# A two-layer hybrid decoder trunk: where the modulation's dots and the softmax sums stand in the order of work

## The chip, the cores and the metric

The kernel runs on one core of a Trainium2 chip. The metric is the device time of one execution in microseconds; the median over several runs counts. Three runs of the kernel before gave 1451.97, 1452.05 and 1452.85 us.

TensorE (PE) multiplies, and transposes by multiplying with the identity. VectorE (DVE) and ScalarE (ACT) do everything between the products. SyncE (SP) issues most of the transfers, GpSimd (POOL) those that add weights in flight. Each engine works off its own queue in order and waits for the others by semaphores.

## The reference

Two layers, 512 positions, width 1024, all in f32. A vector `c` modulates every layer with six vectors of width 1024 (shift, scale and gain, for the mixers and for the feed-forward).

```python
mod = silu(c) @ w_ada + b_ada
sh1, sc1, g1, sh2, sc2, g2 = jnp.split(mod, 6, axis=-1)
h = rmsnorm(x, norm1_w) * (1 + sc1) + sh1
u = h @ w_in                       # pool, conv (u, b, c), q, k, v, three gates
...
o = moba_attention(q, k, v)        # 8 heads of 64, blocks of 256, causal
merged = (gates[:, :, 0] * (y_pool @ p_pool) + gates[:, :, 1] * (y_conv @ p_conv)
          + gates[:, :, 2] * (y_attn @ p_attn))
x = x + g1 * (merged @ w_out)
h2 = rmsnorm(x, norm2_w) * (1 + sc2) + sh2
x = x + g2 * ((silu(h2 @ w_gate) * (h2 @ w_up)) @ w_down)
```

`w_ada` is 1024 by 6144 in each layer. The feed-forward is 2816 wide.

## The kernel before

**Tiling.** Activations lie with features on the 128 partitions and the 512 positions along the free dimension, so a vector of width 1024 is eight tiles. Every f32 product is three matmuls (`mm3`, L159) of a high and a low part: weights arrive by DMA in a raw tile of eight 128 x 128 blocks, ACT rounds them to the high part (`whi`, L327), VectorE subtracts to get the low part (`wlo`, L330). `next_w` (L351) keeps three or four such weight tiles ahead of the one in use. There are three raw buffers, five each of `whi` and `wlo`, and six of a general 4 KB kind, `w4`.

**Stages of a layer.** Input projection; pooling and convolution; K and V; then the attention, which runs in between the products of the first two gates; the third gate and the merging (`GATE2`, with steps "gate j" and "attn j"); the output projection (`tail`, L981); the feed-forward in four parts (`PARTS`), each gate and up products, some of them in pairs (`glu_pair`, L1077) whose weights are sums made by POOL's accumulating transfers into `w4` tiles (`Sums`, L240), and then the down projection, column by column, each ending in a `residual` (L977), `x += product * gain`.

**Dots.** The modulation is not a matmul. For each of the six vectors and each of its eight columns, SP fetches a 128 x 1024 tile of `w_ada` (512 KB) and VectorE multiplies it with silu(c) and sums along the row (`ada_step`, L398, the instruction at L376). `ada_end` (L405) adds the bias to a whole vector. The dots of shift 1 and scale 1 of layer 0 run at the start; the others are tasks with a cost of 1.2 each (0.2 for an `ada_end`) in a queue, `bulk`.

**Order.** Nothing is scheduled at run time: the order of the program is written by three helpers. `mm3` counts columns, and after each 2048 of them (four products of 512 columns) it calls `tick` (L135). A tick steps every fiber that is due and then gives `bulk` a credit of `bulk_rate`; credit is capped at 4.0, and while it is not negative, tasks are taken and charged. `flush_bulk` takes what is left at once. Instructions under `pin` (or `keep_in_program_order`) keep their order; the rest may be moved by the compiler where data and buffers allow. All matmuls, dots and weight splits are pinned.

**Attention.** A fiber, `attention` (L681), goes through four pairs of heads. For each it transposes Q and K (`to_features`) and starts four units, one for each block of 128 queries, `GAP` ticks apart. A `unit` (L582) computes scores, mask, maxima and exponentials, for blocks 2 and 3 separately for keys before and in their own block of 256 (L619 to L639), adds the two sums (L640), takes the reciprocal (L641) and scales the exponentials (L643). After `WAIT` ticks it transposes them and splits the transposes (L654, L655), two ticks later it multiplies with V, and reads the product out (L669 to L674). `tick` steps the attention fiber ahead of the units, as it is first in the list.

**Where the dots stand before.** In layer 0: shift 2 and scale 2 amid the attention, at a rate of 0.27 and in raw buffers (`early=True`); gain 2 in the output projection, at 0.9; then `DOTS = (8, 8, 2, 0)` tasks of layer 1's 36 (scale 1, shift 1, scale 2, shift 2) in the down projections of parts 0 to 3, five more in the last one's tail, and 13 in layer 1's input projection. In layer 1: gain 2 in the output projection. `dots_after` keeps a dot behind the last split of the pair before it.

Of the kernel before, what the change touches and what calls it, by code (L numbers as in the profile page):

```python
# [25 lines left out]
KT = D // P  # L26
# [9 lines left out]
BLOCK = 256  # L36
# [11 lines left out]

SUMS_AHEAD = 4

DOTS = (8, 8, 2, 0)

RAW, BIG = 3, 46

# [25 lines left out]
def hybrid_trunk(ctx, tc, xT, ws, ada, cols, pool_w, qk_w, crow, pos, con, out):  # L80
# [52 lines left out]
            bulk.popleft()[1]()  # L133

    def tick():  # L135
        for f in list(fibers):
            f[0] -= 1
            if f[0] <= 0:
                n = next(f[1], None)
                if n is None:  # L140
                    fibers.remove(f)
                else:
                    f[0] = n
        run_bulk(bulk_rate[0])

    def drain():
        while fibers:
            tick()
# [256 lines left out]
    def ada_end(l, part):  # L405
# [4 lines left out]
        if part == G1:  # L410
            V.tensor_scalar(m, m, 0.5, None, op0=ALU.mult)

    def ada_tasks(l, parts, early=False):
        out = []
        for part in parts:
            for j in range(KT):
                out.append((1.2, lambda part=part, j=j: ada_step(l, part, j, early)))
            out.append((0.2, lambda part=part: ada_end(l, part)))
        return out
# [162 lines left out]
    def unit(hp, i, q, k, v, y, nrq, prq):  # L582

        w = P * (i + 1)

        def scores(o, i, n):
            for z, (qa, ka) in enumerate(((0, 0), (0, 1), (1, 0))):
                for a in range(2):
                    r = slice(a * HD, (a + 1) * HD)
                    matmul(o[:, a], q[qa][r, i * P:(i + 1) * P], k[ka][r, :n], start=(z == 0), stop=(z == 2))  # L590


        if i == 0:
            s = first_two[hp] = ps_pair()
            for u in range(2):
                scores(s[:, :, u * BLOCK:(u + 1) * BLOCK], u, BLOCK)
            diag = s.rearrange("p a (g c) -> p a g c", c=P)[:, :, 0:TT:TT - 1]
            V.tensor_add(diag, diag, mask.unsqueeze(1).unsqueeze(1).to_broadcast([P, 2, 2, P]))
        elif i == 1:
            s = first_two.pop(hp)[:, :, BLOCK:]  # L600
        elif i == 2:

            s, last_one[hp] = ps_pair(), ps_pair()
            for u, o in ((2, s), (3, last_one[hp])):
                scores(o[:, :, :(u + 1) * P], u, (u + 1) * P)
        else:
            s = last_one.pop(hp)
        cell = lambda: sm([P, 2], tag="asm", bufs=16)
        nsc, sc = nrq[:, i, 2 * hp:2 * hp + 2], prq[:, i, 2 * hp:2 * hp + 2]
        m, nb, den = cell(), cell(), cell()  # L610
        pr = [tmp() for _ in range(2)]
        if w <= BLOCK:
            V.tensor_reduce(m, s[:, :, :w], axis=AX.X, op=ALU.max)
            V.tensor_mul(nb, m, nsc)
            for a in range(2):
                A.activation(pr[a][:, :w], s[:, a, :w], AF.Exp, bias=nb[:, a:a + 1],
                             scale=sc[:, a:a + 1], accum_out=den[:, a:a + 1])
        else:

            past, own, diag = s[:, :, :BLOCK], s[:, :, BLOCK:w], s[:, :, i * P:w]  # L620
            gs, under, mp, nbp, d2 = cell(), cell(), cell(), cell(), cell()
            V.tensor_reduce(gs, past, axis=AX.X, op=ALU.add)  # L622
            V.tensor_reduce(mp, past, axis=AX.X, op=ALU.max)  # L623
            for a in range(2):
                V.scalar_tensor_tensor(under[:, a:a + 1], gs[:, a:a + 1], sc[:, a:a + 1], fill,
                                       op0=ALU.mult, op1=ALU.is_lt)
            V.tensor_add(diag, diag, mask.unsqueeze(1).to_broadcast([P, 2, P]))
            V.scalar_tensor_tensor(mp, under, NEG, mp, op0=ALU.mult, op1=ALU.add)
            V.tensor_reduce(m, own, axis=AX.X, op=ALU.max)  # L629
            for a in range(2):  # L630
                V.scalar_tensor_tensor(nb[:, a:a + 1], m[:, a:a + 1], mp[:, a:a + 1], nsc[:, a:a + 1],
                                       op0=ALU.max, op1=ALU.mult)
            V.scalar_tensor_tensor(nbp, under, NEG, nb, op0=ALU.mult, op1=ALU.add)
            for a in range(2):
                A.activation(pr[a][:, BLOCK:w], own[:, a], AF.Exp, bias=nb[:, a:a + 1],  # L635
                             scale=sc[:, a:a + 1], accum_out=den[:, a:a + 1])
            for a in range(2):
                A.activation(pr[a][:, :BLOCK], past[:, a], AF.Exp, bias=nbp[:, a:a + 1],  # L638
                             scale=sc[:, a:a + 1], accum_out=d2[:, a:a + 1])  # L639
            V.tensor_add(den, den, d2)  # L640
        V.reciprocal(den, den)  # L641
        for a in range(2):
            V.tensor_scalar(pr[a][:, :w], pr[a][:, :w], den[:, a:a + 1], None, op0=ALU.mult)  # L643
        yield WAIT[i]

        pt = [None] * 2
        for aa in ([0, 1],) if i < 2 else ([0], [1]):
            n = len(aa)
            tp = ps_mm().rearrange("p (j a q) -> p j a q", a=n, q=P)[:, :i + 1]
            for a in aa:  # L650
                for j in range(i + 1):
                    transpose(tp[:, j, a - aa[0], :], pr[a][:, j * P:(j + 1) * P], ident)
            both = w4([P, i + 1, n, 2, P], F32R)
            A.activation(both[:, :, :, 0], tp, AF.Copy)  # L654
            V.tensor_sub(both[:, :, :, 1], tp, f32(both)[:, :, :, 0])  # L655
            for a in aa:
                pt[a] = both[:, :, a - aa[0]]
        yield 2


        po = (s[:, 0] if i >= 2 else ps_mm()).rearrange("p (a h q) -> p a h q", a=2, h=2)
        for a in range(2):
            for j in range(i + 1):
                matmul(po[:, a].rearrange("p h q -> p (h q)"), v[hp // 2][j][:, hp % 2 * 2 + a].rearrange("p h d -> p (h d)"),
                       pt[a][:, j].rearrange("p h q -> p (h q)"), start=(j == 0), stop=(j == i))
        c = slice(i * P, (i + 1) * P)
        t = tmp()
        part, total = t[:HD, :2 * P].rearrange("p (a q) -> p a q", a=2), t[:, 2 * P:3 * P]
        A.activation(part, po[HD:, :, 0], AF.Copy)  # L669
        V.tensor_add(part, part, po[:HD, :, 1])  # L670
        for a in range(2):
            V.tensor_add(total[a * HD:(a + 1) * HD], part[:, a], po[:HD, a, 0])
        A.activation(y[0][:, c], total, AF.Copy)
        V.tensor_sub(y[1][:, c], total, f32(y[0])[:, c])  # L674
# [65 lines left out]
    for l in range(L):  # L740
# [7 lines left out]
        for n, (k, lo, hi) in enumerate([(k, 0, S) for k in range(KT)] if l == 0 else HALVES + REST):  # L748
# [12 lines left out]
                held[k] = next_w(0 if l == 0 else None)  # L761
            if l > 0 and n == 1:
                second(norm, l, 0, bank)
                bulk.extend(later)
                bulk_rate[0] = 0.75
            w = held[k]
            h = norm.k(k)
            for t in range(lo // P, hi // P):
# [152 lines left out]
            mm3(pp, (pw["h"][:, j, :], pw["l"][:, j, :]), pooled[j], True, True)  # L921
            y_pool.append(split_from(pp, scale=col(C_PS + j)))

        if l == 0:
            bulk.extend(ada_tasks(l, (SC2, SH2), True))
        bulk_rate[0] = 0.27
        ahead_now[0] = 3

        def gate():
# [29 lines left out]
        for step, j in GATE2:  # L959
            if step == "gate":  # L960
                sg2[j] = gate()
                continue
            if j == 0:
                drain()
            if j % 2 == 0:
                aw_ = next_w()
            p1 = ps_mm()
            for z in range(PAIRS):
                mm3(p1, wblk(aw_, 4 * (j % 2) + z), y_attn[z], z == 0, z == PAIRS - 1)
            t = sg2.pop(j)  # L970
            gated(t, p1)
            V.tensor_add(t, t, m01[j])
            merged.append(split_from(t))
        flush_bulk()


        def residual(k, src, lo, hi, part):  # L977
# [50 lines left out]
            return go  # L1028

        ahead_now[0] = 4  # L1030
        bulk.extend(ada_tasks(l, (G2,)))
        bulk_rate[0] = 0.9
        n2 = Norm()
        n2.h = [bigt(F32) for _ in range(KT)]
        table(AF.Abs_reciprocal_sqrt, t[:, 0:1])
# [91 lines left out]
        for part, (along, single, pairs) in enumerate(PARTS):  # L1127
# [25 lines left out]
            bulk_rate[0] = 0.0  # L1153
            for p in range(pairs):
                glu_pair(p == pairs - 1)
            if l + 1 < L:
                if part == 0:
                    later = ada_tasks(l + 1, (SC1, SH1, SC2, SH2))
                n = DOTS[part]
                bulk.extend(later[:n])  # L1160
                del later[:n]
            bulk_rate[0] = 1.5
            blk = Blocks(nk, 4)
            if part + 1 < len(PARTS):
                for n in range(KT):
                    if n == KT // 2:
                        bulk_rate[0] = 0.0
                    o = ps_mm()
                    for k in range(nk):
                        mm3(o, blk(n, k), act[k], k == 0, k == nk - 1)  # L1170
                    residual(n, o, 0, S, G2)
            elif l + 1 == L:
                tail(lambda k: act[k], blk, G2, nk, None, True)
            else:
                flush_bulk()
                drain()
                bulk.extend(later[:5])
                del later[:5]
                bulk_rate[0], credit[0] = 0.8, 0.0
                n1 = Norm()  # L1180
                table(AF.Abs_reciprocal_sqrt, f32(act[-1][1])[:, 0:1])
# [104 lines left out]
```

## Time and profile before

| | us |
|---|---|
| median of three runs | 1452.05 |
| the profiled execution | 1453.0 |
| its span, first to last instruction | 1451.2 |
| PE, matmuls busy | 1442.0 |
| PE, weight loads busy | 1264.8 |
| DVE busy | 1063.1 |
| ACT busy | 663.5 |
| POOL busy | 105.2 |

The stages, by the times from the span's start: input projection of layer 0 from 24, attention and gates 126 to 303, merging 303 to 339, output projection to 388, feed-forward to 726; layer 1's input projection to 799, its attention 838 to 1018, its output projection from 1055, its feed-forward from 1104 to the end.

In the rows of the timeline the columns are: start, busy time, engine, line, operation, output and inputs, shapes, how many instructions were merged, and in brackets the idle time of the engine before it with what ended it. Matmuls overlap, so the distance from one start to the next is their pace, not their busy time. In the rows of the chain the columns are start, length and what it was.

### The profile page before, as it was taken

To read this page: it belongs to the slowest core of one execution; us is meant where nothing else is said; L and a number is where in the kernel's file an instruction comes from. 1 tells how busy PE (TensorE), PEld (TensorE's weight loads), DVE (VectorE), ACT (ScalarE), POOL (GpSimd) and SP (SyncE) were. 2 spreads that over 40 slices of the span, in tenths; PEclk is the share of its full clock that TensorE was granted. 3 is DMA by queue.
4 is the path that set the end of the run, shared out by engine and by line. 5 is a ranking of instruction groups with operands and counts; after the bars stand their busy time and mean duration, and the time that the engine had idled before them with its cause. 6 is when DMAs were issued, how large, how long until landed. Compare 5 with 4: busy or idle time off the path is not lost.

```text
span 1451.2 us, 21838 instructions
## 1 busy us (share of the span) xinstructions
PE 1442.0 (99%) x8379; PEld 1264.8 (87%) x8379; DVE 1063.1 (73%) x1879; ACT 663.5 (46%) x1138; POOL 105.2 (7%) x157
## 2 busy tenths in 40 slices
PE   9999999999999999999999999999999999999998
PEld 7888788888988998989988877888889989989997
DVE  7987888858686767677797776776577757657663
ACT  4634555533553452535444355555335525534450
POOL 0000000001100311210000000000020102111200
PEclk9999999999999999999999999999999999999999
DMA  9644333364436767756545422223473436636432
GB/s 352 223 141 167 124 115 104 117 217 152 100 132 213 196 174 205 187 153 195 190 147 178 151 87 73 73 73 109 153 200 90 135 113 175 174 106 185 131 92 83
DMA packets 84409, 217.18 MB, mean 150 GB/s; under 512 B 10832, under 2 KB 23760, under 8 KB 84304
## 3 DMA queue, kind: packets, MB, share of 16 engines
q1 hardware_dynamic: 67456, 177.37, 35.9%
q0 software_dynamic: 16128, 37.76, 11.8%
q8 instruction: 65, 1.06, 0.3%
q10 hardware_dynamic: 720, 0.66, 0.1%
q14 instruction: 40, 0.33, 0.1%
HBM read 213.65 MB, written 2.10 MB: 149 GB/s over the span
## 4 chain that ended last, share of the span: by engine, by line
PE 92%; DVE 5%; DMA 1%; ACT 1%; issue 1%; SPq 0%; ACTq 0%; DVEq 0%
PE mm L151 78%; PE pair L151 12%; PE mm L157 1%; DVE wlo L330 1%; DMA w<-in_ada 1%; DVE w L376 0%; DVE raw L376 0%; DMA x<-in_xT 0%; DMA raw<-in_ws 0%; DVE tmp L643 0%; DVE asm L622 0%; ACT tmp L638 0%; DVE asm L629 0%; DVE asm L623 0%; ACT tmp L635 0%
## 5 line engine op out<-in xcount | busy, mean ns | idle before, releaser
L151 PE MATMUL mm<-big,whi 128*128 128x512 f32 (+1 forms) x4362 | 1080.2, 339 | 1.7 <-DVE big L938 0.9
L151 PEld LDWEIGHTS mm<-big,whi 128*128 128x128 f32 x4362 | 745.2, 190 | 87.2 <-DVE big L938 1.5
L151 PE MATMUL mm<-big,wlo 128*128 128x512 f32 (+1 forms) x2181 | 736.1, 338 | 0.0
L151 PEld LDWEIGHTS mm<-big,wlo 128*128 128x128 f32 x2181 | 413.8, 190 | 44.5
L327 ACT ACTIVATE whi<-raw 128x1024 fp32r<-128x1024 f32 (+2 forms) x240 | 248.9, 1040 | 265.7 <-PE mm L151 190.2
L330 DVE TENSOR_TENSOR wlo<-raw,whi 128x1024 fp32r<-128x1024 f32 (+2 forms) x240 | 283.9, 1192 | 50.5 <-ACT whi L327 47.7
L327 ACT ACTIVATE whi<-w 128x1024 fp32r<-128x1024 f32 x72 | 76.2, 1058 | 148.1 <-PE mm L151 85.3
L978 DVE SCALAR_TENSOR_TENSOR x<-mm,mod,x 128x512 f32<-128x512 f32 (+1 forms) x90 | 61.7, 689 | 78.1 <-PE mm L151 77.9
L256 POOL DMA_DIRECT2D w<-in_ws x72 | 46.3, 656 | 951.6 <-issue 294.1
L330 DVE TENSOR_TENSOR wlo<-w,whi 128x1024 fp32r<-128x1024 f32 x72 | 86.7, 1221 | 31.6 <-ACT whi L327 30.9
L376 DVE SCALAR_TENSOR_TENSOR w<-w,csil 128x1024 f32<-128x1024 f32 x80 | 95.9, 1220 | 16.9 <-DMA w<-in_ada 16.8
L151 PE MATMUL pair<-whi,big 128*128 128x512 f32 x224 | 76.8, 390 | 0.0
L258 POOL DMA_DIRECT2D w<-in_ws x72 | 64.0, 897 | 157.8 <-DMA w<-in_ws 142.6
L151 PE MATMUL pair<-big,whi 128*128 128x256 f32 (+1 forms) x376 | 74.0, 294 | 0.0
L151 PEld LDWEIGHTS pair<-big,whi 128*128 128x128 f32 x376 | 60.4, 191 | 2.2
L151 PE MATMUL mm<-whi,big 128*128 128x512 f32 x160 | 57.2, 394 | 1.4 <-ACT big L501 1.1
L151 PE MATMUL pair<-big,wlo 128*128 128x256 f32 (+1 forms) x188 | 55.3, 294 | 0.0
L938 DVE SCALAR_TENSOR_TENSOR big<-big,mm 128x512 f32<-128x512 f32 x48 | 32.5, 683 | 28.6 <-PE mm L151 28.5
L151 PEld LDWEIGHTS pair<-whi,big 128*128 128x128 f32 x224 | 42.1, 188 | 8.8
L515 DVE TENSOR_TENSOR big<-tmp,big 128x512 fp32r<-128x512 f32 x48 | 33.1, 691 | 21.4 <-ACT big L514 20.4
L514 ACT ACTIVATE big<-tmp 128x512 fp32r<-128x512 f32 x48 | 29.9, 622 | 36.2 <-DVE tmp L1120 12.8
L151 PE MATMUL pair<-wlo,big 128*128 128x512 f32 x112 | 43.6, 390 | 0.0
(190 smaller groups left out, 1238.5 us busy)
## 6 DMA issues: line engine op xcount, KB each, us to landing
raw<-in_ws SPq DMA_DIRECT2D x146, 512.0 KB, 3.3
w<-in_ada SPq DMA_DIRECT2D x80, 512.0 KB, 4.9
w<-in_ws POOLq DMA_DIRECT2D x144, 256.0 KB, 4.7
raw<-in_ws SPq DMA_DIRECT2D x64, 256.0 KB, 3.8
raw<-in_ws SPq DMA_DIRECT2D x24, 384.0 KB, 3.5
raw<-in_ada SPq DMA_DIRECT2D x16, 512.0 KB, 3.3
raw<-in_ws SPq DMA_DIRECT2D x16, 448.0 KB, 5.1
raw<-in_ws SPq DMA_DIRECT2D x36, 128.0 KB, 2.8
```

Source lines behind the costliest of these rows:

```text
L151: tc.keep_in_program_order(T.matmul(*a, **k))
L157: tc.keep_in_program_order(T.transpose(*a))
L256: nc.gpsimd.dma_start(dst, self.source(0, 1))
L258: nc.gpsimd.dma_start(dst, self.source(*other), accum_op=ALU.add)
L327: A.activation(hi[:, :n], raw[:, :n], AF.Copy)
L330: ins = V.tensor_sub(lo[:, :n], raw[:, :n], f32(hi)[:, :n])
L376: return V.scalar_tensor_tensor(aw, aw, 1.0, csil, op0=ALU.mult, op1=ALU.mult, accum_out=mod[l][:, part, j:j + 1])
L514: A.activation(hi, src, AF.Copy)
L515: last_split[0] = V.tensor_sub(lo, src, f32(hi))
L938: V.scalar_tensor_tensor(sg, sg, 1.0, branch, op0=ALU.add, op1=ALU.mult)
L978: V.scalar_tensor_tensor(x[k][:, lo:hi], src, mod[l][:, part, k:k + 1], x[k][:, lo:hi], op0=ALU.mult, op1=ALU.add)
```

## The change

Four things. The dots of shift 2 and scale 2 leave layer 0's attention and layer 1's input projection; in both layers they start with the step "attn 0" of the merging, behind `drain`, at a rate of 0.85 and in `w4` buffers, and run on into the output projection. The dots of gain 2 leave the output projection; in both layers they become single columns, `g2_column`, each with its own bias add on ACT: three behind the pair of feed-forward part 0 and one ahead of each of the next five columns of its down projection. With 18 tasks of layer 1 instead of 36, `DOTS` becomes (0, 9, 4, 0), and the last five go into the last tail. In a unit for query blocks 2 and 3, two ticks pass between the exponentials and L640 (now pinned), and one instead of three between the scaling and the transposes. `tick` serves the first fiber, the attention, last.

```diff
-DOTS = (8, 8, 2, 0)
+DOTS = (0, 9, 4, 0)
...
     def tick():
-        for f in list(fibers):
+
+        for f in fibers[1:] + fibers[:1]:
             f[0] -= 1
...
+    def g2_column(l, j):
+
+        ada_step(l, G2, j, False)
+        m = mod[l][:, G2, j:j + 1]
+        A.activation(m, m, AF.Identity, bias=colt[:, l, C_ADA + G2 * KT + j:C_ADA + G2 * KT + j + 1])
...
                 A.activation(pr[a][:, :BLOCK], past[:, a], AF.Exp, bias=nbp[:, a:a + 1],
                              scale=sc[:, a:a + 1], accum_out=d2[:, a:a + 1])
-            V.tensor_add(den, den, d2)
+
+            yield 2
+            pin(V.tensor_add(den, den, d2))
         V.reciprocal(den, den)
         for a in range(2):
             V.tensor_scalar(pr[a][:, :w], pr[a][:, :w], den[:, a:a + 1], None, op0=ALU.mult)
-        yield WAIT[i]
+        yield WAIT[i] - (2 if w > BLOCK else 0)
...
                 second(norm, l, 0, bank)
-                bulk.extend(later)
-                bulk_rate[0] = 0.75
...
-        if l == 0:
-            bulk.extend(ada_tasks(l, (SC2, SH2), True))
-        bulk_rate[0] = 0.27
+        bulk_rate[0] = 0.0
         ahead_now[0] = 3
...
             if j == 0:
                 drain()
+                bulk.extend(ada_tasks(l, (SC2, SH2)))
+                bulk_rate[0] = 0.85
...
             merged.append(split_from(t))
-        flush_bulk()
...
         ahead_now[0] = 4
-        bulk.extend(ada_tasks(l, (G2,)))
-        bulk_rate[0] = 0.9
...
                 glu_pair(p == pairs - 1)
+            if part == 0:
+                for j in range(3):
+                    g2_column(l, j)
             if l + 1 < L:
                 if part == 0:
-                    later = ada_tasks(l + 1, (SC1, SH1, SC2, SH2))
+                    later = ada_tasks(l + 1, (SC1, SH1))
...
                         bulk_rate[0] = 0.0
+                    if part == 0 and n + 3 < KT:
+                        g2_column(l, n + 3)
                     o = ps_mm()
...
                 flush_bulk()
                 drain()
-                bulk.extend(later[:5])
-                del later[:5]
+                bulk.extend(later)
```

## The prediction

> **What bounds the kernel now.** I read the page first, its busy shares, costliest groups and DMA issues, then the windows by stage, then the timeline at each place where TensorE shows a pause.
>
> ```profile
> span 1451.2 us, 21838 instructions
> PE 1442.0 (99%) x8379; PEld 1264.8 (87%) x8379; DVE 1063.1 (73%) x1879; ACT 663.5 (46%) x1138; POOL 105.2 (7%) x157
> ...
> L376 DVE SCALAR_TENSOR_TENSOR w<-w,csil 128x1024 f32<-128x1024 f32 x80 | 95.9, 1220 | 16.9 <-DMA w<-in_ada 16.8
> w<-in_ada SPq DMA_DIRECT2D x80, 512.0 KB, 4.9
> ```
>
> TensorE is the bound, and its matmuls are untouched by the change. So VectorE work is worth nothing by itself; only those places count where TensorE stands still for it. A dot (L376) costs 1.22 us of VectorE and a transfer of 512 KB, 4.9 us from issue to landing. The windows by stage (columns: length, then busy time of PE, PEld, DVE, ACT, POOL, then clock, DMA share, GB/s) say where such places can be:
>
> ```profile
> 126.00:303.00 177.00, 176.06 (x913) 144.30 (x912) 144.10 (x336) 92.72 (x211) 0.00 (x0) 1.00 0.38 127
> 303.00:339.00 36.00, 36.00 (x161) 29.79 (x160) 22.56 (x33) 11.96 (x17) 0.00 (x0) 1.00 0.47 168
> 339.00:388.00 49.00, 49.00 (x273) 42.96 (x272) 35.92 (x59) 18.81 (x29) 8.75 (x12) 1.00 0.56 158
> 749.00:795.00 46.00, 46.00 (x205) 38.08 (x204) 36.86 (x59) 18.43 (x27) 0.31 (x1) 1.00 0.56 196
> 838.00:1018.00 180.00, 178.39 (x922) 145.58 (x921) 128.51 (x308) 95.47 (x215) 0.00 (x0) 1.00 0.25 86
> ```
>
> In the two attention stages (126 to 303 and 838 to 1018) TensorE loses 0.94 and 1.61 us by this count; in the merging (303 to 339), the output projection behind it, and the input projection of layer 1 (749 to 795) it loses nothing. The change can gain in the attention alone, a few microseconds at most. Everywhere else it can only lose.
>
> **What it removes.** Layer 0's wait, seen in the timeline:
>
> ```profile
> 145.44 1.22 DVE L376 SCALAR_TENSOR_TENSOR raw<-raw,csil 128x1024 f32<-128x1024 f32 x1
> ...
> 159.03 0.75 DVE L643 TENSOR_SCALAR tmp<-tmp,asm 128x384 f32<-128x384 f32 x2
> ...
> 160.86 0.49 PE L157 MATMUL mm<-ident,tmp 128*128 128x128 f32 x3
> ...
> 161.22 0.57 DVE L672 TENSOR_TENSOR tmp<-tmp,mm 64x128 f32<-64x128 f32 x2
> ...
> 161.94 0.52 PE L157 MATMUL mm<-ident,tmp 128*128 128x128 f32 x3 [0.58 <-DVE tmp L672]
> ...
> 162.81 0.74 PE L151 MATMUL mm<-big,whi 128*128 128x512 f32 x2 [0.35 <-ACT big L933]
> ```
>
> Six transposes take from 160.86 to 162.81, 1.95 us. Their second half needs a PSUM buffer that L672 has to read out first, and the next matmul one that ACT's L933 frees, itself queued behind what follows L672. VectorE is late because it is hardly idle from the dot at 145.44 on. Layer 1, without dots, runs the same piece in 875.47 - 874.90 = 0.57 us (next fence). So the first term is 1.95 - 0.57 = 1.38 us. The second half is late by 161.94 - 160.86 - 0.57 / 2 = 0.8 us. The dot taken out (1.22) is more than that alone, and L643 (0.75) moves too, so I take the whole of it.
>
> Layer 1's waits:
>
> ```profile
> 874.90 0.81 PE L157 MATMUL mm<-ident,tmp 128*128 128x128 f32 x6
> ...
> 875.47 0.70 PE L151 MATMUL mm<-big,whi 128*128 128x512 f32 x2
> ...
> 876.24 0.62 PE L151 MATMUL mm<-big,whi 128*128 128x512 f32 x2
> ...
> 876.71 0.40 PE L151 MATMUL mm<-big,wlo 128*128 128x512 f32 x1
> ...
> 877.17 0.16 DVE L640 TENSOR_TENSOR asm<-asm,asm 128x2 f32<-128x2 f32 x1 [1.91 <-ACT tmp L638]
> 877.25 0.68 DVE L938 SCALAR_TENSOR_TENSOR big<-big,mm 128x512 f32<-128x512 f32 x1
> ...
> 877.98 0.73 PE L151 MATMUL mm<-big,whi 128*128 128x512 f32 x2 [0.88 <-DVE big L938]
> 878.55 0.40 PE L151 MATMUL mm<-big,wlo 128*128 128x512 f32 x1
> ...
> 960.99 0.16 DVE L640 TENSOR_TENSOR asm<-asm,asm 128x2 f32<-128x2 f32 x1 [0.70 <-ACT tmp L638]
> ...
> 961.95 0.60 PE L157 MATMUL mm<-ident,w 128*128 128x128 f32 x4
> 962.18 1.02 DVE L655 TENSOR_TENSOR w<-mm,w 128x384 fp32r<-128x384 f32 x2
> ...
> 962.79 0.72 PE L151 MATMUL mm<-big,whi 128*128 128x512 f32 x2 [0.24 <-DVE w L655]
> ```
>
> This is the wait that the delayed sum is made for. L640 stands at the head of VectorE's queue for 1.91 us, until ACT's exponentials (L638) are done; L938 stands behind it, and a matmul needs the buffer that L938 frees. The pace without a wait is (876.71 - 876.24) / 2 = 0.235 us a matmul, here it is 877.98 - 876.71 = 1.27: a loss of 1.03. The pair behind the wait is slow too: 878.55 - 877.98 = 0.57 against 0.47, another 0.10. At 962 it is the same pattern: L640 waits 0.70, L641 and L643 run behind it, and L655, which frees the transposes' buffer, comes late. Four transposes take 0.84 (961.95 to 962.79); undisturbed they take 0.38:
>
> ```profile
> 839.83 0.63 PE L157 MATMUL mm<-ident,w 128*128 128x128 f32 x4 [0.27 <-DVE big L909]
> ...
> 840.21 0.70 PE L151 MATMUL mm<-big,whi 128*128 128x512 f32 x2
> ```
>
> a loss of 0.46. Sum removed: 1.38 + 1.03 + 0.10 + 0.46 = 2.97 us. The wait for L909 in this last fence belongs to the evacuation of V and is not touched.
>
> **What it adds and moves.** (a) *Sums two steps later.* No instruction is added. A step is four mm3 calls, 12 x 0.235 = 2.8 us of TensorE; the sums keep one step ahead of the transposes that need them, and last 962.18 - 960.99 = 1.2 us, from L640 to what follows L643. The pinned L640 then waits for exponentials issued two steps ago, so it is ready, and the weight splits behind it do not wait. Cost 0 if VectorE is less than 2.8 - 1.2 = 1.6 us behind its program at that step; if it is further behind, rival 1. Serving old units first moves their transposes ahead of new scores inside one step: nothing by itself, the condition is the same.
>
> (b) *16 dots into the merging, both layers.* VectorE has room early and none late there:
>
> ```profile
> 316.05 3.72 DVE L330 TENSOR_TENSOR wlo<-raw,whi 128x1024 fp32r<-128x1024 f32 x3
> 325.79 0.69 DVE L938 SCALAR_TENSOR_TENSOR big<-big,mm 128x512 f32<-128x512 f32 x1 [6.02 <-PE mm L151]
> ...
> 331.23 1.22 DVE L330 TENSOR_TENSOR wlo<-raw,whi 128x1024 fp32r<-128x1024 f32 x1
> ...
> 339.38 0.69 DVE L938 SCALAR_TENSOR_TENSOR big<-big,mm 128x512 f32<-128x512 f32 x1 [0.17 <-PE mm L151]
> ...
> 340.82 1.37 DVE L515 TENSOR_TENSOR big<-big,big 128x512 fp32r<-128x512 f32 x2
> ```
>
> The credit of the bulk queue is at its cap of 4.0 when the dots enter (rate 1.4 with an empty queue before), so with a cost of 1.2 a dot and a rate of 0.85 a step four dots fall into the first step, one each into steps 2, 4 and 5, and with attn 2 to 7 (steps 7 to 12) come steps 7, 8, 10 and 11, four more; the last five fall into the first columns of the output projection, where the eight G2 dots that stood there are gone. The dots of steps 1 to 8 can run in the idle time before 325.79 (6.02 us). The two of steps 10 and 11 follow the split at 331.23, where VectorE is full: 2 x 1.22 = 2.44 us. Behind them stands L515 of column 7, which ends at 340.82 + 1.37 = 342.2. TensorE ends attn 7 at 339.4, and reads that tile's low half after seven products of three matmuls and one matmul more, 22 x 0.227, at 344.4 (the pace is from the chain's rows in (c)). The slack is 2.2, so 0.24 us is lost. Lower bound 0 (dots run earlier), upper bound all four in the full stretch: 4.9 - 2.2 = 2.7. I take 0.3 a layer, 0.6 in all, because the tick arithmetic is fixed by the code.
>
> (c) *G2 dots as single columns in feed-forward part 0.* Four are pinned ahead of the splits of the third to fifth weight tile:
>
> ```profile
> 451.09 0.69 DVE L515 TENSOR_TENSOR big<-tmp,big 128x512 fp32r<-128x512 f32 x1 [0.70 <-ACT big L514]
> 451.70 3.48 DVE L330 TENSOR_TENSOR wlo<-raw,whi 128x1024 fp32r<-128x1024 f32 x3
> 455.11 1.22 DVE L376 SCALAR_TENSOR_TENSOR w<-w,csil 128x1024 f32<-128x1024 f32 x1
> ...
> 462.25 1.23 DVE L376 SCALAR_TENSOR_TENSOR w<-w,csil 128x1024 f32<-128x1024 f32 x1 [1.63 <-DMA w<-in_ada]
> ```
>
> ```profile
> 432.58 49.95 PE mm L151 x288
> ...
> 485.40 17.33 PE mm L151 x144
> ```
>
> Half of the 288 matmuls are the pair's (17.33), the other half the down projection: it starts at 432.58 + 17.33 = 449.9 and goes at 32.6 / 144 = 0.227 us a matmul, so its third tile of 24 is due 48 x 0.227 later, at 460.8. Four dots from 451.8 end at 456.6, that split at 457.9: 2.9 us to spare, if the four transfers have landed. If two of them wait for a buffer (first dot done at 453.0, second at 454.1, plus 4.9) it ends about at 461.4, when the low half is read at 461.25: 0.2. Before, the third dot's transfer, free to start when the first dot ended (456.3), held it until 462.25: 5.9, with which it is 1.2. Bounds 0 and 1.2 a layer; I take 0, since the SP queue fetches dots long ahead where buffers are free. The bias adds on ACT have 12 us before the column's residual.
>
> (d) The 13 dots that leave layer 1's input projection leave a stage without waits: 0. Parts 1 to 3 of layer 0 get 9, 4 and 5 tasks for 8, 2 and 5: 0, as the dots beside part 0 stopped nothing (fence above, one unbroken piece).
>
> Sum: -2.97 + 0.6 = -2.4 us. Against the profiled execution (1453.0, of which 1451.2 are the span) that gives 1450.6; the median of the runs is 0.95 below that execution, so **1449.6**.
>
> [...]
>
> **The rivals.** 1. *Scaling too late.* If VectorE is over 1.6 us behind at the step of the sums, the transposes wait. The sums of block 3 fall into the step that attends for block 2: a split (1.22), a gating (0.68) and L672 (0.57) ahead of them make 2.5, 0.9 over, in the 8 units of block 3 7.2 us: 1452.05 - 2.4 + 7.2 = 1456.9. For it: VectorE is 81% busy in layer 0's attention; against: that share falls by 16 x 1.22 us, to 70%. 8%.
> 2. *Full stretch in the merging.* All four dots sit ahead of column 7's L515, in both layers: 5.4 instead of 0.6, 1454.5. It decides from 2.2 us of lateness on, and passes the gain at 3.7. For it: nothing in the code keeps a dot behind the older splits; against: the idle 6.02 us. 12%.
> 3. *Columns late in part 0*: 2 x 1.2 = 2.4, 1452.1. For it: two free buffers at a time would do that; against: what (c) says of the early fetch. 10%.
> 4. *It does not do what it says in layer 0*: the backlog at 161 is the reduces' own and 1.38 us stay; 1451.0. For it: the softmax of block 3 stands in the same queue; against: layer 1 has it too, and no wait there. 15%.
>
> **How the numbers follow.** The forecast has 55%; its own range is 1448.3 (no cost of (b), and some of the untouched V waits gone by a shift) to 1451.0. A measurement of this kernel tells 0.2%, 2.9 us, from no change: faster than 1449.15 is somewhat over half of the forecast's 55%, 0.32. Over 1454.95 is rival 1, and half of rival 2, if a late transfer joins it: 0.15. The rest, 0.53, is within. The range 1448.2 to 1454.6 leaves out rival 1, the worse half of 2 and a little below.
>
> **What would show it.** Right: no dot between 126 and 303; L640 with no wait for L638; no TensorE pause where 161, 876 and 962 were; one unbroken piece of TensorE through the merging. Wrong: a TensorE wait for L643 or tmp at the transposes (rival 1), for L515 or L972 at the start of the output projection (2), for wlo behind L376 after part 0's pair (3), for L672 in layer 0's first head pair (4).

## The result, and the profile after

The changed kernel takes 1477.28 us (median of 5 runs, 1475.51 to 1479.98) where the kernel before takes 1452.05 (1451.61 to 1452.95): a ratio of 1.0173, 95% interval 1.0162 to 1.0185. It is slower by 25 us, where 2.4 us of gain was forecast. The profiled execution took 1478.85 us, against 1453.0 before: 25.85 us to account for.

The page of the changed kernel, span and busy shares. Lines have moved: the sums L640, L641, L643 are now L649, L650, L652; the exponentials L645 (the last of a unit); the read-out of a unit L678 to L683; the splits of weights L331; the dot L377; the gating L943; the split of the merged columns L521 and L522; the matmul L152 and the transpose L158.

```profile
span 1477.1 us, 21858 instructions
PE 1449.8 (98%) x8379; PEld 1268.7 (86%) x8379; DVE 1065.0 (72%) x1877; ACT 669.8 (45%) x1154; POOL 105.4 (7%) x157
```

VectorE and ScalarE do the same work as before to within 7 us, and TensorE the same 8379 matmuls. So the 26 us of span are mostly pauses of TensorE. Its view of waits names their place (engine and what waited, what it waited for: us in total, times, longest us); the same view of the kernel before has no row for L643, the scaling:

```profile
PE mm L158 <- DVE tmp L652: 16.8, 12, 2.3
PE mm L158 <- ACT tmp L645: 2.4, 2, 1.2
...
PE mm L152 <- ACT big L521: 1.1, 2, 0.5
...
PE mm L152 <- DVE big L522: 0.4, 2, 0.2
```

The first two rows are transposes that stand still until their probabilities are scaled: 14 waits, all of blocks 2 and 3 but a short one (0.2 us) at 141.75. In the two of the second row the view names exponentials (L645), which end within 0.1 us of the scaling. This view counts from the modelled end of the matmul ahead. Counted from start to start, less what the same pair of shapes usually takes, TensorE loses 11.8 us there in layer 0 and 9.7 in layer 1, together 21.6. The windows by stage agree (columns as in the prediction):

```profile
126.00:303.00 177.00, 166.41 (x834) 134.88 (x833) 124.26 (x296) 87.24 (x200) 0.00 (x0) 0.97 0.23 81
...
853.00:1043.00 190.00, 181.34 (x933) 147.74 (x932) 130.69 (x311) 96.47 (x217) 0.00 (x0) 1.00 0.24 82
```

In the first 177 us of layer 0's attention there were 913 matmuls before and are 834 now, with 166.41 us of TensorE busy against 176.06, and VectorE is *less* busy than before, 124.26 against 144.10. It is not overloaded, it waits. Layer 1's attention (853 to 1043) loses 8.66 us by this count, where it lost 1.61. The mean clock of 0.97 in the first row is a second loss, taken up below.

One of the waits in the timeline of the changed kernel (start, duration, engine, line and operation; in brackets the idle time ahead of it and what ended it). First ScalarE, the unit's last exponentials, then VectorE and TensorE:

```profile
210.31 0.57 ACT L645 ACTIVATE tmp<-pair,asm,nrq 128x256 f32<-128x256 f32 x1
210.76 0.21 ACT L645 ACTIVATION_READ_ACCUMULATOR tmp<-pair,asm,nrq 128x1 f32 x1
```

```profile
213.79 0.75 DVE L525 SCALAR_TENSOR_TENSOR big<-mm,colt,big 128x512 fp32r<-128x512 f32 x1 [3.85 <-ACT big L524]
...
217.00 0.41 DVE L679 TENSOR_TENSOR tmp<-tmp,pair 64x256 f32<-64x256 f32 x1 [2.46 <-ACT tmp L678]
...
218.72 0.28 DVE L683 TENSOR_TENSOR big<-tmp,big 128x128 fp32r<-128x128 f32 x1
...
218.92 0.15 DVE L649 TENSOR_TENSOR asm<-asm,asm 128x2 f32<-128x2 f32 x1
218.99 1.22 DVE L331 TENSOR_TENSOR wlo<-raw,whi 128x1024 fp32r<-128x1024 f32 x1
...
219.30 0.39 PE L152 MATMUL mm<-big,wlo 128*128 128x512 f32 x1
220.13 0.15 DVE L650 RECIPROCAL asm<-asm 128x2 f32<-128x2 f32 x1
...
220.79 0.87 DVE L652 TENSOR_SCALAR tmp<-tmp,asm 128x512 f32<-128x512 f32 x2
...
221.41 1.06 PE L158 MATMUL mm<-ident,tmp 128*128 128x128 f32 x8 [1.72 <-DVE tmp L652]
```

The exponentials are done at 210.76 + 0.21 = 210.97. Their sum L649 runs at 218.92, 7.95 us later, and VectorE stands idle for 3.85 us up to 213.79 (2.82 of them after the exponentials) and for another 2.46. It could have added two columns at any time there, but in its queue L649 stands behind L683, the end of the *older* unit's read-out, and that chain begins with ScalarE's L678, which waits for TensorE's attend (2.83 us idle up to 216.59). The first idle time is for L525, ahead of it in the same queue, which waits for ScalarE's L524. Then a weight split of 1.22 us slips in between L649 and L650. TensorE's last matmul started at 219.30, the transposes at 221.41: 2.11 - 0.23 = 1.88 us lost.

### The profile page after: what moved, and what is told of

Same layout as the page of the kernel before. It is cut to its first block, busy times and chain, and to the rows that moved or that the text cites. A ratio compares the mean times of both kernels' runs of the same rounds, so it can differ in the third digit from the quotient of the medians.

```text
span 1477.1 us, 21858 instructions
## 1 busy us (share of the span) xinstructions
PE 1449.8 (98%) x8379; PEld 1268.7 (86%) x8379; DVE 1065.0 (72%) x1877; ACT 669.8 (45%) x1154; POOL 105.4 (7%) x157
## 5 line engine op out<-in xcount | busy, mean ns | idle before, releaser
L152 PE MATMUL mm<-big,whi 128*128 128x512 f32 (+1 forms) x4362 | 1084.4, 340 | 1.5 <-ACT big L521 1.1
L152 PEld LDWEIGHTS mm<-big,whi 128*128 128x128 f32 x4362 | 747.5, 190 | 90.8 <-issue 2.9
L152 PE MATMUL mm<-big,wlo 128*128 128x512 f32 (+1 forms) x2181 | 737.4, 338 | 0.0
L152 PEld LDWEIGHTS mm<-big,wlo 128*128 128x128 f32 x2181 | 414.7, 190 | 44.6
L331 DVE TENSOR_TENSOR wlo<-raw,whi 128x1024 fp32r<-128x1024 f32 (+2 forms) x240 | 284.0, 1193 | 64.3 <-ACT whi L328 64.1
L377 DVE SCALAR_TENSOR_TENSOR w<-w,csil 128x1024 f32<-128x1024 f32 x96 | 115.2, 1220 | 12.0 <-DMA w<-in_ada 11.7
L331 DVE TENSOR_TENSOR wlo<-w,whi 128x1024 fp32r<-128x1024 f32 x72 | 86.8, 1221 | 32.0 <-ACT whi L328 31.3
L152 PE MATMUL pair<-whi,big 128*128 128x512 f32 x224 | 76.7, 389 | 0.0
L152 PE MATMUL pair<-big,whi 128*128 128x256 f32 (+1 forms) x376 | 74.0, 294 | 0.0
L152 PEld LDWEIGHTS pair<-big,whi 128*128 128x128 f32 x376 | 60.4, 191 | 2.2
L152 PE MATMUL mm<-whi,big 128*128 128x512 f32 x160 | 57.1, 394 | 1.5 <-ACT big L508 1.1
L152 PE MATMUL pair<-big,wlo 128*128 128x256 f32 (+1 forms) x188 | 55.3, 294 | 0.0
L152 PEld LDWEIGHTS pair<-whi,big 128*128 128x128 f32 x224 | 42.1, 188 | 8.6
L522 DVE TENSOR_TENSOR big<-tmp,big 128x512 fp32r<-128x512 f32 x48 | 33.1, 690 | 21.5 <-ACT big L521 20.5
L521 ACT ACTIVATE big<-tmp 128x512 fp32r<-128x512 f32 x48 | 30.0, 624 | 34.3 <-DVE tmp L1124 12.8
L943 DVE SCALAR_TENSOR_TENSOR big<-big,mm 128x512 f32<-128x512 f32 x48 | 32.5, 684 | 17.3 <-PE mm L152 15.6
L152 PE MATMUL pair<-wlo,big 128*128 128x512 f32 x112 | 43.6, 390 | 0.0
```

Source lines behind the costliest of these rows:

```text
L152: tc.keep_in_program_order(T.matmul(*a, **k))
L331: ins = V.tensor_sub(lo[:, :n], raw[:, :n], f32(hi)[:, :n])
L377: return V.scalar_tensor_tensor(aw, aw, 1.0, csil, op0=ALU.mult, op1=ALU.mult, accum_out=mod[l][:, part, j:j + 1])
L521: A.activation(hi, src, AF.Copy)
L522: last_split[0] = V.tensor_sub(lo, src, f32(hi))
L943: V.scalar_tensor_tensor(sg, sg, 1.0, branch, op0=ALU.add, op1=ALU.mult)
```

## The experiments

Three theories stood at the start. **The sums**: two steps on and pinned they come too late for their transposes (rival 1 of the prediction). **The order** of serving units does it, since older units' read-outs now go first. **The dots**, in the merging or beside part 0, do it. Of the first there were two forms, that the delay itself is too long, or that the pin is what holds the sum back. Each ratio is against the kernel before, timed again beside that run (medians of 1452.17 to 1453.34 us), so it is the ratios that compare.

**Each of the three undone or done alone.** The sums put back:

```diff
-            yield 2
-            pin(V.tensor_add(den, den, d2))
+            V.tensor_add(den, den, d2)
...
-        yield WAIT[i] - (2 if w > BLOCK else 0)
+        yield WAIT[i]
```

> The changed kernel with the softmax of blocks 2 and 3 put back in one step (no two steps between exponentials and sums, no pin on the sum), dots and order of the fibers as changed. Theory A (the transposes wait for the late sums and scaling, about 21 us of waits on L652 and some 4 us of halved clock behind them): both go, only the two waits of 1.2 us at the end of the merging stay, so about 1452 to 1454 us. Theory B (the order of the fibers or the moved dots make the waits): stays above 1470 us.

Measured 1454.98 us, ratio 1.0011 (1.0001 to 1.0020), span 1453.1: by the ratios, 23.5 us of the 25 are gone. The reverse, only the sums two steps on and pinned in the kernel before (the same lines, the other way):

> The kernel before with the delayed and pinned sums alone; dots and fiber order as before. Theory A: the waits of the transposes on the scaling are all there without the other parts, and VectorE is fuller in layer 0 by the 16 dots, so 1472 to 1482 us. Theory B: within 3 us of 1452.

Measured 1475.44, ratio 1.0152 (1.0137 to 1.0167). With dots and order untouched nearly the whole loss is there. Its view of waits of TensorE, where L645 is the scaling and L638 the exponentials:

```profile
PE mm L157 <- DVE tmp L645: 15.9, 14, 2.6
PE mm L157 <- ACT tmp L638: 2.9, 2, 1.8
```

The order put back in the changed kernel:

```diff
-        for f in fibers[1:] + fibers[:1]:
+        for f in list(fibers):
```

> The changed kernel with the attention fiber served first again. If serving the units under way first does it (the transposes come at the start of the step instead of behind the scores), most of the 25 us go, below 1460 us. If the delay of the sums does it, the transposes of block 2, which share a step with no scores, wait as before and the time stays at 1470 to 1480 us.

Measured 1473.35, ratio 1.0141 (1.0126 to 1.0156): the loss stays, so the order isn't its cause. The two ratios differ by 0.0032, about 4.6 us. That is not assigned: the two rows of waits make 16.7 us in its view where they make 19.2 in the changed kernel's, and its profile has no stretch of halved clock (mean 1.0) where the changed kernel's (0.997) has three (below). The kernel before with nothing but the new order:

> The kernel before with nothing but the new order of serving units. If the order costs 0.11 us a head pair, 1452 + 1.8 = 1453.8 us; if it also takes some of L1's waits at 876 (0.57 of 1.03 us went where it was in force), about 1453.2. If it is free: 1451.5 to 1452.2.

Measured 1453.59, ratio 1.0005 (0.9996 to 1.0013): nothing that can be told apart. Only the dots moved (sums and order both back):

> Only the moved dots (sums and order of the fibers as before). The dots leave layer 0's attention (about 1.4 us gained at its first pair of heads) and cost 1.2 us at the end of the merging in each layer: 1452 to 1455 us, and layer 1's two waits at L640 (1.0 and 0.5 us) are there. If the order of the fibers matters, it differs from the kernel with the sums put back by more than 1 us.

Measured 1455.18, ratio 1.0018 (1.0009 to 1.0027). That is a small loss, looked into further down.

**Delay or pin.** The sums two steps on, but free to stand anywhere:

```diff
-            pin(V.tensor_add(den, den, d2))
+            V.tensor_add(den, den, d2)
```

> The changed kernel without the pin on the delayed sum. If the pin does it (the sum may not pass the weight split before it), the waits on L652 go and about 1453 us are left. If the place in the program does it (the sum comes behind the read-out of the older unit, which stands waiting in VectorE's queue for ACT and TensorE, and one step ahead of the transposes), 1468 to 1478 us.

Measured 1455.63, ratio 1.0015 (1.0006 to 1.0024): without the pin the delay costs nothing that can be told from the kernel with the sums back. Its timeline at the same unit:

```profile
209.03 0.16 DVE L649 TENSOR_TENSOR asm<-asm,asm 128x2 f32<-128x2 f32 x1 [1.83 <-ACT tmp L645]
...
209.43 0.49 DVE L652 TENSOR_SCALAR tmp<-tmp,asm 128x512 f32<-128x512 f32 x1
...
211.28 0.41 DVE L679 TENSOR_TENSOR tmp<-tmp,pair 64x256 f32<-64x256 f32 x1 [0.32 <-ACT tmp L678]
```

Left to itself the schedule puts the sum where it stood before the change, ahead of L679, right when the exponentials are done. It undid the two steps, with the wait of 1.83 us at the head of VectorE's queue that they were to end. The other way round, pinned with no step between:

```diff
-            yield 2
             pin(V.tensor_add(den, den, d2))
...
-        yield WAIT[i] - (2 if w > BLOCK else 0)
+        yield WAIT[i]
```

> The changed kernel with the pinned sum directly behind the exponentials, with no step between: the pin without the delay. If the delayed pin is what costs (the sum tied two steps nearer to its transposes and behind the read-out of the older unit), the pin three steps ahead of them costs little: 1453 to 1457 us, no TensorE wait for L652's scaling over 0.5 us. If a pinned sum costs wherever it stands, since it holds VectorE's queue until ACT's exponentials are done (1.91 us where it was seen), 1465 us or more.

Measured 1454.89, ratio 1.0013 (1.0004 to 1.0022): the pin by itself costs nothing either. And pinned, one step on (`yield 1`, `WAIT[i] - 1`):

> The changed kernel with the pinned sums one step after the exponentials instead of two, two steps ahead of the transposes. Theory C (the pin holds the sum at its place in the program, behind the read-out of the older unit, and that place is too near the transposes): one step, 2.8 us, more room is more than the longest wait of 2.5 us, so the waits on the scaling are under 3 us in all and the time is 1453 to 1459 us. Rival (any pinned sum costs, since a weight split of 1.2 us gets between it and the reciprocal): over 1465 us.

Measured 1454.75, ratio 1.0018 (1.0009 to 1.0027). At the same unit:

```profile
208.58 0.16 DVE L649 TENSOR_TENSOR asm<-asm,asm 128x2 f32<-128x2 f32 x1 [1.16 <-ACT tmp L645]
...
208.98 0.88 DVE L652 TENSOR_SCALAR tmp<-tmp,asm 128x512 f32<-128x512 f32 x2
...
210.82 0.41 DVE L679 TENSOR_TENSOR tmp<-tmp,pair 64x256 f32<-64x256 f32 x1 [0.30 <-ACT tmp L678]
```

One step on, the pinned place is still ahead of the read-out; two steps on it is behind it. The same over all 16 sums, worked out from VectorE's and ScalarE's records (how many stand right behind the last instruction of a read-out; time from the end of the unit's last exponential to the sum, median and longest):

```
kernel                               behind a read-out     median us   longest us
before                                   1 of 16              0.03        0.94
after (pinned, two steps on)            14 of 16              4.78       12.88
only the sums (pinned, two steps on)    16 of 16              7.35       10.68
order back (pinned, two steps on)       16 of 16              7.13       10.74
two steps on, not pinned                 0 of 16              0.03        2.23
pinned, one step on                      0 of 16              0.03        1.41
pinned, no step                          0 of 16              0.03        0.17
```

In the changed kernel the 16 sums wait 91.3 us in all behind their exponentials, and VectorE is idle for 25.0 of these; the rest is work that stands ahead of them.

So it takes both, the pin and the two steps: the three kernels that have both lose 20 to 25 us, the five with the moved dots that lack one or both (sums back, only the dots, not pinned, one step, no step) lie within 1.0011 to 1.0018 of the kernel before. Why the pinned place lies behind the read-out is read from the code only: pinned instructions keep their order among themselves, and in the step two on, the attend's pinned matmuls of the older unit come first.

**What stays: 2 us with the dots.** The kernels that lose nothing at the scaling are still above the kernel before. All five show the same two waits at the start of each output projection. The timeline of the changed kernel there:

```profile
354.71 1.22 DVE L377 SCALAR_TENSOR_TENSOR w<-w,csil 128x1024 f32<-128x1024 f32 x1
...
355.86 1.28 DVE L943 SCALAR_TENSOR_TENSOR big<-big,mm 128x512 f32<-128x512 f32 x2
357.05 1.29 DVE L979 TENSOR_TENSOR big<-big,big 128x512 f32<-128x512 f32 x2
...
357.77 0.64 ACT L521 ACTIVATE big<-big 128x512 fp32r<-128x512 f32 x1 [1.67 <-DVE big L979]
...
358.43 1.28 ACT L175 ACT_TABLE_LOAD   x1
...
359.56 0.39 PE L152 MATMUL mm<-big,wlo 128*128 128x512 f32 x1
...
359.83 0.61 ACT L521 ACTIVATE big<-big 128x512 fp32r<-128x512 f32 x1
360.48 0.69 DVE L522 TENSOR_TENSOR big<-big,big 128x512 fp32r<-128x512 f32 x1 [1.34 <-ACT big L521]
...
360.50 0.50 PE L152 MATMUL mm<-big,whi 128*128 128x512 f32 x1 [0.55 <-ACT big L521]
...
361.22 0.50 PE L152 MATMUL mm<-big,whi 128*128 128x512 f32 x1 [0.22 <-DVE big L522]
```

The late dot at 354.71 holds the gating of columns 6 and 7 back, and between the two splits of ScalarE (L521) its table load slips in, 1.28 us, though the second one's input, the second L979, is done at 358.34. The last L521 ends at 360.44, its L522 at 361.17, and TensorE needs them at once. From start to start the two matmuls come 360.50 - 359.56 - 0.23 = 0.71 and 361.22 - 360.50 - 0.23 = 0.49 late: 1.2 us a layer. To test it, the dots are let in early and kept out from column 2 to the output projection, with no pin:

```diff
-                bulk_rate[0] = 0.85
+                bulk_rate[0] = 1.3
+            if j == 2:
+                bulk_rate[0] = 0.0
...
         ahead_now[0] = 4
+        bulk_rate[0] = 1.0
         n2 = Norm()
```

> The changed kernel without the pin, and with no dots in attn 2 to 7: a rate of 1.3 up to there, 0, and 1.0 from the output projection on. If the two waits at the end of the merging come from the dots ahead of the last splits, both go (2.4 us): 1450 to 1453 us, at or below the kernel before. If ACT's table load makes them by itself, they stay and it is 1454 to 1456 us.

Measured 1452.65, ratio 1.0003 (0.9994 to 1.0012). The same with the sums fully back:

> The changed kernel with the sums put back in one step, and the same spread of the dots: 1450 to 1453 us by the same reasoning; it differs from the one without the pin by the sums alone, under 1 us.

Measured 1451.99, ratio 1.0000 (0.9991 to 1.0009), span 1450.4. In both, TensorE's waits for L521 and L522 are gone, and the splits of the last two columns run ahead of the table load, here in the second:

```profile
339.68 1.29 ACT L521 ACTIVATE big<-big 128x512 fp32r<-128x512 f32 x2
340.99 1.28 ACT L175 ACT_TABLE_LOAD   x1
```

The ratios fell by 0.0012 and 0.0011, about 1.7 us, where the two waits make 2.4; the intervals allow both.

**Looking for a version that beats both.** Spread dots and the old order, once with pinned sums one step on, once with the sums as before:

> The changed kernel with pinned sums one step on, units served in the old order, and the merging's dots at rate 1.3 until column 2, none until the output projection. If the merging's two waits (2 x 1.2 us) and the small pauses behind the scores (0.11 us per head pair, some 16 pairs) are the only costs left, 1451 to 1452 us; TensorE does not wait at the start of the output projection. If the order costs nothing by itself: 1452 to 1453.

> Sums as before (one step, no pin), units served in the old order, merging's dots spread: what stays of the change is only where the dots run. Terms: L0's wait at 161 gone (1.38 us), L1's at 876 and 962 as before, no wait at the output projection, nothing else: 1450.7 us, 1.4 below the kernel before. A rival has the pauses of the old order back in other places: 1452.

Measured 1452.36, ratio 0.9994 (0.9986 to 1.0003), and 1452.20, ratio 0.9997 (0.9988 to 1.0006). Both intervals hold 1: no version here is shown to be faster than the kernel before. The second was expected 1.4 us below it and is 0.4 below by its ratio. Its profile shows a pause in layer 0's attention that the kernel before doesn't have (nor do the kernels above with the new order); it ends at 248.63, and the one with only the dots moved has it too, up to 247.89. Its row in the view of waits, the same in both:

```profile
PE mm L157 <- ACT big L935: 0.7, 1, 0.7
```

So with the old order the move of the dots gives back there a part of what it gains at 161. What the order is worth stays open, too: neither these nor the order alone separates 0 from the 1.8 us that the expectation for the order puts on small pauses behind the scores.

## Why the prediction was wrong

**The step that failed is (a)**, "The pinned L640 then waits for exponentials issued two steps ago, so it is ready", with its cost of 0 "if VectorE is less than 2.8 - 1.2 = 1.6 us behind its program". It took load as the only thing that could make VectorE late. The sum was ready, but not first: its own queue held it behind a read-out that waits for TensorE and ScalarE, up to 12.88 us after its exponentials, with VectorE idle for more than a quarter of the time that the sums waited. The condition that decides is what stands ahead of the pinned instruction, and what *that* waits for. The prediction counted what stands ahead of the sum as work alone (the 2.5 us of rival 1), and did not ask what that work waits for.

**Rival 1** named the right symptom, TensorE waiting for the scaling, and had 8%. Its price was 0.9 us in 8 places, 7.2; measured were 14 waits of 1.5 us on average, 21.6, in both layers and for both blocks. Its reason, VectorE behind by 2.5 us of work ahead of the sums, is at most a part of it: VectorE was less busy than before.

**The clock** was no term of the sum at all. Behind three of the 14 waits the granted clock was 0.50, in each case for 3.42 us. The changed kernel's windows and TensorE's rows there:

```profile
207.54:210.96 3.42, 3.42 (x12) 2.94 (x12) 2.37 (x6) 2.67 (x9) 0.00 (x0) 0.50 0.23 74
211.04:214.46 3.42, 3.42 (x18) 2.84 (x17) 0.67 (x1) 2.24 (x3) 0.00 (x0) 1.00 0.19 74
```

```profile
205.09 0.39 PE L152 MATMUL mm<-big,wlo 128*128 128x512 f32 x1
207.37 1.37 PE L158 MATMUL mm<-ident,tmp 128*128 128x128 f32 x6 [1.90 <-DVE tmp L652]
...
209.82 1.05 PE L152 MATMUL mm<-big,whi 128*128 128x512 f32 x2
210.67 0.53 PE L152 MATMUL mm<-big,wlo 128*128 128x512 f32 x1
211.04 0.63 PE L152 MATMUL mm<-big,whi 128*128 128x512 f32 x2
211.51 0.39 PE L152 MATMUL mm<-big,wlo 128*128 128x512 f32 x1
```

After a gap of 2.28 us between starts (205.09 to 207.37) the matmuls go at (210.67 - 209.82) / 2 = 0.425 us each, then again at (211.51 - 211.04) / 2 = 0.235. By these two paces 3.42 us hold 8 matmuls that lose 0.19 each, 1.5 in all; by the clock of 0.50 it is half of 3.42, 1.7. My estimate is 1.6 for each stretch, 4.8 for the three.

**(b) was mis-sized.** It named the column, the split and the place, and gave 0.3 us a layer; measured were 1.2, well inside its bounds of 0 and 2.7. What was missing, as its timeline reads, is the table load that came between the two L521, since they no longer stood side by side; with the dots spread, the load runs behind both and the waits are gone. **(c) and (d) were right**: the view of TensorE's waits has no row for a weight tile or a dot, so rival 3 did not happen. **What it removes** was right in layer 0: with the sums back, the six transposes at 161 take 162.64 - 162.04 = 0.60 us instead of 1.95, so 1.35 of the forecast 1.38 are gained; with only the dots moved they take 162.02 - 161.45 = 0.57. Rival 4 is false:

```profile
162.04 0.82 PE L158 MATMUL mm<-ident,tmp 128*128 128x128 f32 x6
162.64 0.72 PE L152 MATMUL mm<-big,whi 128*128 128x512 f32 x2
```

In layer 1 it was right too. The waits at 876 and 962 were to go by the sums' delay, and where the sums are pinned two steps on they are gone: TensorE's view of waits has no row for the gating or for the splits behind the transposes in the changed kernel (L943, L664), nor in the one with only the sums moved (L940, L657). Where the sums stay in their old place, waits stay. The first row is of the kernel with only the dots moved, where the wait at 876 is unshortened. The second is of the one with the sums back and the new order: 0.48 us late from start to start, and another wait at 967 is 0.96 late, about as much together as the two in the kernel before.

```profile
878.56 0.73 PE L151 MATMUL mm<-big,whi 128*128 128x512 f32 x2 [0.88 <-DVE big L940]
```

```profile
878.11 0.73 PE L152 MATMUL mm<-big,whi 128*128 128x512 f32 x2 [0.31 <-DVE w L662]
```

Together: 21.6 (scaling) + 4.8 (clock) + 2.4 (merging) - 1.35 (layer 0) - 1.6 (layer 1) = 25.85, against 25.85 between the two profiled executions. So close a fit is luck: the clock's term is an estimate, and small waits that no term names differ too, such as 0.8 us for L909 at 838 to 840 that only the kernel before has. The gain of the sums' delay was as forecast; its price was the term put at nothing.

## What to carry to other kernels

An instruction that is pinned to a later place is not "ready and free": it waits for all that stands ahead of it in its engine's queue, as the sum did here for 7.95 us with its exponentials done. Before moving one, list what stands ahead of the new place and follow each of those back to the engine it waits for; if one of them hangs on the very engine that the moved instruction feeds, the slack is gone, however idle the engine looks. And where TensorE is 99% busy, as here, price a pause of 2.28 us at up to 3.9: behind two such pauses and one of 2.69 the clock was 0.50 for 3.42 us, an estimated 1.6 more.

## What the runs showed of the hardware

A wait can be followed by a halved clock, but isn't always. In the changed kernel the clock was 0.50 in 207.54 to 210.96, 255.33 to 258.75 and 299.70 to 303.12. The gaps there, between starts, were 2.28 us (above), 2.28 (251.88 to 254.16) and 2.69 (297.08 to 299.77). Its longest wait, 2.31 us up to 936.48, a gap of 2.70 between starts, left the clock at 1.00 (934.58 to 938.00 and on to 941.40). In the kernel with the old order the same transposes as at 207.37, after 207.08 - 205.00 = 2.08 us, ran on at full speed:

```profile
205.00 0.39 PE L151 MATMUL mm<-big,wlo 128*128 128x512 f32 x1
207.08 0.85 PE L157 MATMUL mm<-ident,tmp 128*128 128x128 f32 x6 [1.69 <-DVE tmp L651]
...
208.46 0.62 PE L151 MATMUL mm<-big,whi 128*128 128x512 f32 x2
208.92 0.39 PE L151 MATMUL mm<-big,wlo 128*128 128x512 f32 x1
```

(208.92 - 208.46) / 2 = 0.23 us a matmul. So the length of the gap alone does not decide it: 0.50 came behind 2.28 us in two places, and 1.00 stayed behind 2.70 in another. What decides is not shown here.

Slow matmuls also come in places outside the change. At the start of the kernel TensorE waits for ScalarE's first conversion, 1.11 us in the kernel before, but 1.98 in the profile with only the order changed, and behind it the matmuls started 0.43 us apart (19.24 to 19.67), about the 0.425 measured above at a clock of 0.50:

```profile
18.67 0.77 PE L152 MATMUL mm<-whi,big 128*128 128x512 f32 x1 [1.98 <-ACT big L502]
19.24 0.63 PE L152 MATMUL mm<-wlo,big 128*128 128x512 f32 x1
19.67 0.65 PE L152 MATMUL mm<-whi,big 128*128 128x512 f32 x1
```

That is 0.9 us of wait, and from the first of these to the next matmul on `mm` with `big` and `whi` it takes 23.11 - 18.67 = 4.44 us, where the kernel before takes 21.17 - 17.89 = 3.28: 1.2 more. The 2.0 us together, in a place that the edit does not touch, are nearly the 2.4 that were forecast as gain: single profiles can't rank these versions, only the ratios of many runs.
